# A diffusion layer with recurrence, long convolution and experts: equal column pieces, and gates as single fp32 products

## The chip, the cores and the metric

One core of one Trainium2 chip. The time is device microseconds (us) of one execution, the median of three: 927.65 us for the kernel before (925.95 to 929.68). Engines: PE multiplies matrices (its weight loads are shown as PEld), DVE and ACT work on elements, POOL too, SP issues the transfers (DMA).

## The reference

One layer over 512 latent tokens and 256 context tokens of width 1024, all in fp32:

- RMSNorm with shift and scale from the conditioning, then a projection into two head groups.
- A bidirectional gated recurrence over 512 channels. Two gates, r and i, are sigmoids of 64x64 block products of the convolved input u. With `log_a = -8 * r * softplus(-lam)`: `a = exp(log_a)`, `b = sqrt(-expm1(2 * log_a)) * (i * u)`, and the state is `h = a * h + b`, forward and backward, first over the context, then over the latents.
- A Hyena group: two long convolutions, done as transforms.
- Norms, an output projection, a gated residual, and a second RMSNorm.
- A mixture of experts: top group of 4, in it the top 2 of 8 experts; each expert is `(silu(t @ w_gate) * (t @ w_up)) @ w_down`, with 1024 x 512 weights. Then a residual and the last RMSNorm.

## The kernel before

The program is written in one order and recorded; a planner (`Recorder.order`) then lays every instruction on its engine by a list schedule with costs of its own, 25 passes, and keeps the order with the shortest planned end. So the order on an engine isn't that of the source, and a change of a few instructions lays all of it out anew. Copies and simple products may be put on one of two engines (`X`, the class `Either`). Buffers are fixed in the order of the source: an arena of 103 cells of 256 columns (`take`), and 12 slots of 2048 columns for rounded operands (`takeR`); `give` returns them.

Ahead of the experts stand, in the planner's order: filters, the conditioning products (`mod_group`, 32 columns wide), the norm, the recurrence (`lru_pair`, twice, for two blocks of 128 channels each), gelu, the convolutions (`order`, `long_conv`), the output projection and the routing.

In `lru_pair` the gates need more accuracy than one fp32r product gives, so weights and input are split into a rounded part and a remainder (`lwH`, `lwL`, and `st`, named `vst`), and each product is three fp32r products. There are 16 gates (4 blocks, 2 directions, r and i), each in two parts of 256 and 512 columns. The square root of 1 - a^2 comes from tanh: `ncoef` scales r so that 1 - a^2 = tanh(..) * (1 + a^2), and `q` holds a^2.

The experts are sorted by load; each gets a fixed number of places (`CAPS`: three of 64, then 192, 128, 128, 96, nine of 64, fifteen of 32, one of 0). A unit packs chunks of 64 or 32 tokens side by side into the 128 columns of PE: two 64s, four 32s, or, mixed, one 64 and two 32s. Two of the units are mixed: the one of the expert with 96 places (its chunks of 64 and 32, and another expert's 32; the last H of `ORDER = "MMHMQHQAMHQ"`, behind two units that are put first), and the last M. A is a group of two units of two 64s; Q is a unit of four 32s. In `product` each piece is one fp32 product per step, on its strip of columns; an order edge (`before`) keeps the pieces of a unit in sequence in the plan:

```
for i, (k, kk, h) in enumerate(parts):
    for (p0, w), wv in zip(sub[0], sub[2]):
        o = T.matmul(b[p0:p0 + w, :nc_], lhs[:, k, p0:p0 + w], wv(m, kk, h)[:, c0:c0 + nc_], ...
```

A unit has 8 steps of gate, 8 of up and 4 of down for each of two halves of the output. Before them its tokens are gathered (bf16 products with `R`), behind them the result is scattered and added to `x2`. The weights come in loads of 1 MB (`load`, issued at L1818 on the queue of SP) into a ring of buffers, in the order of use, six loads an expert; a load waits until PE has done with what its buffer held. The first three experts don't depend on the routing, all others do (`eid`).

Of the kernel before, what the change touches and what calls it, by code (L numbers as in the profile page):

```python
# [13 lines left out]
F32 = mybir.dt.float32  # L14
# [4 lines left out]
OP = mybir.AluOpType  # L19
# [658 lines left out]
class Arena:  # L678
# [9 lines left out]
    def take(self, name, shape, top=False, step=1):  # L688
        n = math.prod(shape)
        m = -(-n // 256)  # L690
        best = None
        for o in range(0, self.n - m + 1, step):
            if any(self.used[o:o + m]):
                continue
            key = -o if top else (max(self.stamp[o:o + m]), o)
            if best is None or key < best[0]:
                best = (key, o)
        if best is None:
            raise RuntimeError(f"arena: no room for {name} ({m} cells), {self.used.count(False)} free; "
                               + ", ".join(f"{k}@{o}+{c}" for k, (o, c) in self.live.items()))  # L700
        o = best[1]
        self.used[o:o + m] = [True] * m
        self.peak = max(self.peak, sum(self.used))
        self.clock += 1
        key = f"{name}.{self.clock}"
        self.live[key] = (o, m)
        v = View.of(self.mem)[:, o * 256:o * 256 + n]
        if len(shape) > 1:
            names = "abcdef"[:len(shape)]
            v = v.rearrange(f"p ({' '.join(names)}) -> p {' '.join(names)}", **dict(zip(names, shape)))  # L710
        v.key, v.home, v.since = key, self, max(self.stamp[o:o + m])
        return v
# [30 lines left out]
def kernel(ctx: ExitStack, tc: tile.TileContext, a: dict, out: bass.AP, dbg=None):  # L743
# [29 lines left out]
    take = AR.take  # L773
# [5 lines left out]
    def give(*vs):  # L779
        for v in vs:  # L780
            v.home.give(v)
# [7 lines left out]
    def ps():  # L789
        if REC.direct:  # L790
            nbank[0] += 1
            return View.of(Mem((128, 512), F32, banks[nbank[0] % 8]))
        return View.of(Mem((128, 512), F32, bank=-1))
# [382 lines left out]
    V.tensor_scalar(t8[0], t8[0], 0.0, 0.5, op0=OP.max, op1=OP.mult)  # L1176
    V.tensor_tensor(t8[4], t8[4], t8[0], op=OP.add)
    V.tensor_scalar(coef, t8[4], -16.0, None, op0=OP.mult)
    V.tensor_scalar(ncoef, t8[4], 16.0, None, op0=OP.mult)


    def split(src, wh, wl):

        X.copy(wh, src)
        X.tensor_tensor(wl, src, wh.bitcast(F32), op=OP.subtract)
# [27 lines left out]
    for i in range(2):  # L1213
# [3 lines left out]
        for h in range(2):  # L1217
            split(st[:, 2 * h:2 * h + 2], *(w[:, 2 * h:2 * h + 2] for w in UW[i]))
        give(st)
    lwH, lwL = (takeR("lw", [16, 128]) for _ in range(2))  # L1220
    split(lw, lwH, lwL)
    give(lw)
    ct = [take("ct", [512]) for _ in range(2)]
    for j in range(2):
        b = ps()
# [7 lines left out]
    give(*cH, *cL)  # L1233

    def lru_pair(blks):
        vs, sts = {}, {}
        for bk in blks:
            bc = ps()
            for j in range(2):
                T.transpose(bc[:, 128 * j:128 * j + 128], ct[j][:, 128 * bk:128 * bk + 128], ident)  # L1240
            bl = ps()
            for k in range(8):
                wh, wl = (w[:, k % 4, 128 * bk:128 * bk + 128] for w in UW[k // 4])
                h, l = (t[k // 4][:, k % 4] for t in (hH, hL))
                T.matmul(bl, wh, h, start=k == 0, stop=False)
                T.matmul(bl, wh, l, start=False, stop=False)
                T.matmul(bl, wl, h, start=False, stop=k == 7)
            v = take("v", [768])
            for b, o0, n in ((bc, 0, 256), (bl, 256, 512)):
                X.copy(v[:, o0:o0 + n], b[:, :n], bias=col("cab", bk), scale=col("caw", 8 + bk))  # L1250
                for k, d0, s0, m in ((0, 2, 0, n - 2), (1, 1, 0, n - 1), (3, 0, 1, n - 1)):
                    V.scalar_tensor_tensor(v[:, o0 + d0:o0 + d0 + m], b[:, s0:s0 + m], col("caw", 4 * k + bk),
                                           v[:, o0 + d0:o0 + d0 + m], op0=OP.mult, op1=OP.add)
            vs[bk] = v
        if blks[-1] == 3:
            give(*UW[0], *UW[1], *ct)
        for bk, v in vs.items():
            st = sts[bk] = takeR("vst", [2048], late=True)
            X.copy(st[:, :768], v)
            X.tensor_tensor(st[:, 768:1536], v, st[:, :768].bitcast(F32), op=OP.subtract)  # L1260
        its = [(bk, d) for bk in blks for d in range(2)]
        rt, it = {}, {}
        for bk, d in its:
            for m, (dst, bn) in enumerate(((rt, "ba"), (it, "bx"))):
                g = take("g", [768])
                gi = (d * 2 + m) * 4 + bk
                b1, b2 = ps(), ps()
                for b, c0, n in ((b1, 0, 256), (b2, 256, 512)):
                    for j, (w, o) in enumerate(((lwH, 0), (lwH, 768), (lwL, 0))):
                        T.matmul(b[:, :n], w[:, gi], sts[bk][:, o + c0:o + c0 + n], start=j == 0, stop=j == 2)  # L1270
                S.activation(g[:, :256], b1[:, :256], AF.Sigmoid, bias=col(bn, 4 * d + bk))
                S.activation(g[:, 256:], b2, AF.Sigmoid, bias=col(bn, 4 * d + bk))
                dst[bk, d] = g
        give(*sts.values())
        at, bt = {}, {}
        for bk, d in its:
            X.tensor_tensor(it[bk, d][:], it[bk, d][:], vs[bk][:], op=OP.mult)
        give(*vs.values())
        for bk, d in its:
            at[bk, d] = take("at", [768])  # L1280
            S.activation(at[bk, d][:], rt[bk, d][:], AF.Exp, scale=coef[:, 4 * d + bk:4 * d + bk + 1])
            S.activation(rt[bk, d][:], rt[bk, d][:], AF.Tanh, scale=ncoef[:, 4 * d + bk:4 * d + bk + 1])
            q = take("q", [768])
            X.tensor_tensor(q[:], at[bk, d][:], at[bk, d][:], op=OP.mult)
            V.scalar_tensor_tensor(rt[bk, d][:], q[:], 1.0, rt[bk, d][:], op0=OP.add, op1=OP.mult)
            give(q)
        for bk, d in its:
            S.activation(rt[bk, d][:], rt[bk, d][:], AF.Sqrt)
            X.tensor_tensor(rt[bk, d][:], rt[bk, d][:], it[bk, d][:], op=OP.mult)
        for bk in blks:  # L1290
            hf, hb = it[bk, 0], it[bk, 1]
            A_, B_ = at[bk, 0], rt[bk, 0]
            V.tensor_tensor_scan(hf[:], A_[:], B_[:], 0.0, op0=OP.mult, op1=OP.add)
            A_, B_ = at[bk, 1], rt[bk, 1]
            V.tensor_tensor_scan(hb[:, 255::-1], A_[:, 255::-1], B_[:, 255::-1], 0.0, op0=OP.mult, op1=OP.add)
            V.tensor_tensor_scan(hb[:, 767:255:-1], A_[:, 767:255:-1], B_[:, 767:255:-1], hb[:, 0:1],
                                 op0=OP.mult, op1=OP.add)
            X.tensor_tensor(rnn[:, bk], hf[:, 256:], hb[:, 256:], op=OP.add)
        for bk, d in its:
            give(rt[bk, d], it[bk, d], at[bk, d])  # L1300
# [177 lines left out]
    while left:  # L1478
        k = left.pop(0)
        i = int(k[1:] or 0)  # L1480
        if k[0] == "L":
            lru_pair((i, i + 1))
            if not [x for x in left if x[0] == "L"]:
                give(lwH, lwL)
        elif k[0] == "M":
            (mod_second, mod_third)[i - 1]()
        elif k[0] in "vab":
            project(*{"v": ("v", 1024, 0), "a": ("g0", 1536, 4), "b": ("g1", 2048, 8)}[k[0]], i)
        elif k[0] in "CD":
            order("CD".index(k[0]), i)  # L1490
            if not [x for x in left if x[0] in "CD"]:
                give(dff, dfi)
        elif k == "W":
            for h in range(WOE):
                wos[h, 0] = load_wo(h, 0)
        elif k == "X":
            load_x2()
        elif k[0] == "G":
            gelu_pair((i, i + 1))
        if not [x for x in left if x[0] in "LvabG"] and k[0] in "LvabG":  # L1500
            give(*hH, *hL)
# [350 lines left out]
    def expert_units(subs, need=lambda m: None, then=lambda: None, last=False):  # L1852
# [16 lines left out]

        def product(sub, m, lhs, parts, c0=0, nc_=512):  # L1870
            b, before = ps(), None
            for i, (k, kk, h) in enumerate(parts):
                for (p0, w), wv in zip(sub[0], sub[2]):
                    o = T.matmul(b[p0:p0 + w, :nc_], lhs[:, k, p0:p0 + w], wv(m, kk, h)[:, c0:c0 + nc_], start=i == 0,
                                 stop=i == len(parts) - 1, tile_position=(0, p0), skip_group_check=True)
                    if not REC.direct:

                        if before is not None:
                            o.preds.setdefault(before, None)
                        before = o.i  # L1880
            return b
# [155 lines left out]
```

## Time and profile before

| | |
|---|---|
| median of three runs | 927.65 us (925.95 to 929.68) |
| profiled execution | 931.36 us; its span 929.6 us |
| busy share of PE, DVE, ACT, POOL | 92%, 55%, 30%, 3% |
| moved by DMA | 259.73 MB, mean 279 GB/s |
| mean granted clock of PE | 0.971 |

A row of a group view names the line (that of a helper here: L560 for all plain operations, L567 for those that may go to either engine), the engine, the operation, output and inputs, for PE rows and columns of the weights, then the shape and the count; behind the bar the busy time in us, the mean of one in ns, and the idle time before them. An fp32 product on PE leaves two records in the trace, an fp32r or bf16 product one. Records of fp32r carry f32 in the view; those on slots with 128x128 weights are fp32r.

### The profile page before, as it was taken

The numbers are of one execution on the slowest core, as the hardware profiler recorded it, in microseconds if no ns is written. First come the engines' busy times: TensorE is split into PE (matmuls) and PEld (weight loads), VectorE is DVE, ScalarE is ACT, GpSimd is POOL, SyncE is SP. The second block draws the span as 40 slices with busy tenths as digits, with TensorE's granted clock in tenths as the row PEclk, the third lists the DMA queues.
The fourth block names the chain that finished last, engine by engine and source line by source line (L and its number), as shares of the span: only waits on it lengthen the run. The fifth ranks groups of instructions, "written<-read, shape, count | busy, mean of one in ns | idle before, by whom it ended". The sixth has DMA issues, their size and how long they took to land.

```text
span 929.6 us, 13429 instructions
## 1 busy us (share of the span) xinstructions
PE 855.6 (92%) x5282; PEld 453.6 (49%) x5283; DVE 507.3 (55%) x971; ACT 279.9 (30%) x511; POOL 23.6 (3%) x25
## 2 busy tenths in 40 slices
PE   3988998899999799599999999999999999999984
PEld 0344674578887577435544444453554323233332
DVE  7989889599999977604233322431413214212135
ACT  4678188764345124301211110120110100000014
POOL 0000001010003000000000000000000000000002
PEclk9989999799999899799999999999999999999997
DMA  9985377333423596398999989999999999876693
GB/s 292 414 276 195 103 238 218 135 118 120 148 80 131 187 327 223 119 361 306 367 386 386 386 294 359 388 386 386 386 387 386 386 387 382 321 281 223 231 335 142
DMA packets 132618, 259.73 MB, mean 279 GB/s; under 512 B 6928, under 2 KB 28432, under 8 KB 129606
## 3 DMA queue, kind: packets, MB, share of 16 engines
q1 hardware_dynamic: 132534, 258.81, 77.7%
q8 instruction: 43, 0.70, 0.3%
q14 instruction: 25, 0.20, 0.1%
q10 hardware_dynamic: 16, 0.02, 0.0%
HBM read 252.49 MB, written 6.31 MB: 278 GB/s over the span
## 4 chain that ended last, share of the span: by engine, by line
PE 68%; DVE 7%; DMA 1%; ACT 1%; issue 0%; SPq 0%; DVEq 0%; ACTq 0%
PE bank L560 68%; DVE arena L567 2%; DVE slot L567 2%; DVE arena L560 2%; DMA slot<-in_w_down_dram 1%; DVE slot L560 1%; ACT slot L560 0%; DVE R L560 0%; DVE rsb_in L560 0%; DVE fine L560 0%; ACT arena L560 0%; ACT slot L567 0%; SPq L1818 0%; DVE finy L560 0%; DVE hy L560 0%
## 5 line engine op out<-in xcount | busy, mean ns | idle before, releaser
L560 PE MATMUL bank<-arena 128*64 128x512 f32 (+8 forms) x1434 | 314.6, 533 | 26.0 <-DMA arena<-in_b_ada_dram 5.9
L560 PE MATMUL bank<-slot 128*128 128x512 f32 (+1 forms) x1064 | 282.8, 410 | 14.9 <-DVE slot L567 4.8
L560 PE MATMUL bank<-slot,arena 128*64 128x512 f32 (+2 forms) x936 | 242.9, 597 | 1.9 <-DMA slot<-in_w_down_dram 0.9
L560 PEld LDWEIGHTS bank<-slot 128*128 128x128 f32 x1064 | 195.2, 193 | 99.5 <-issue 27.3
L560 PEld LDWEIGHTS bank<-arena 128*32 128x32 f32 (+5 forms) x1434 | 100.5, 132 | 166.8 <-issue 117.5
L560 DVE TENSOR_TENSOR arena<-arena,bank 128x512 f32<-128x512 f32 (+2 forms) x131 | 80.5, 663 | 167.4 <-PE bank L560 167.2
L567 DVE TENSOR_TENSOR arena<-arena 128x512 f32<-128x512 f32 (+3 forms) x142 | 120.6, 886 | 2.5 <-DMA arena<-in_w_dram 1.8
L560 PEld LDWEIGHTS bank<-slot,arena 128*64 128x64 f32 (+1 forms) x936 | 58.3, 124 | 111.6 <-issue 101.0
L560 ACT ACTIVATE arena<-bank 128x512 f32<-128x512 f32 (+1 forms) x66 | 38.3, 595 | 243.4 <-PE bank L560 240.8
L560 PEld LDWEIGHTS <-slot 128*128 128x128 bf16 x1344 | 76.9, 98 | 40.9 <-issue 40.6
L560 PE MATMUL bank<-R,slot 128*128 128x128 bf16 x1344 | 88.7, 220 | 0.3 <-ACT arena L567 0.3
L567 DVE TENSOR_SCALAR arena<-bank,A2c,B2c 128x128 f32<-128x128 f32 x36 | 14.6, 410 | 115.6 <-PE bank L560 115.5
L567 ACT ACTIVATE arena<-bank,B2c,A2c 128x128 f32<-128x128 f32 x76 | 30.7, 454 | 137.1 <-DVE arena L567 85.4
L560 ACT ACTIVATE slot<-arena 128x512 fp32r<-128x512 f32 (+2 forms) x43 | 27.7, 645 | 113.5 <-DVE arena L560 104.2
L560 DVE SCALAR_TENSOR_TENSOR arena<-bank,iw,arena 128x512 f32<-128x512 f32 (+1 forms) x29 | 21.2, 732 | 69.6 <-PE bank L560 69.2
L560 PE MATMUL bank<-ident,arena 128*128 128x128 f32 (+2 forms) x234 | 40.7, 292 | 5.2 <-ACT arena L567 2.2
L560 ACT ACTIVATE arena<-arena 128x512 f32<-128x512 f32 (+6 forms) x59 | 32.7, 589 | 26.5 <-DVE arena L560 21.4
L560 PEld LDWEIGHTS bank<-ident,arena 128*128 128x128 f32 (+2 forms) x234 | 30.2, 160 | 19.9 <-issue 5.7
L567 ACT ACTIVATE slot<-slot 128x1024 fp32r<-128x1024 f32 (+1 forms) x32 | 26.4, 846 | 28.4 <-DVE slot L567 22.9
L567 DVE TENSOR_TENSOR slot<-slot 128x1024 fp32r<-128x1024 f32 (+1 forms) x35 | 33.7, 974 | 0.1
L560 ACT ACT_TABLE_LOAD x23 | 29.5, 1283 | 6.0 <-DMA arena<-in_pack_dram 4.6
L560 DVE TENSOR_TENSOR arena<-bank,arena 128x512 f32<-128x512 f32 (+1 forms) x42 | 27.7, 680 | 5.5 <-PE bank L560 3.1
(172 smaller groups left out, 417.3 us busy)
## 6 DMA issues: line engine op xcount, KB each, us to landing
arena<-in_w_down_dram SPq DMA_DIRECT2D x41, 1024.0 KB, 13.5
slot<-in_w_up_dram SPq DMA_DIRECT2D x39, 1024.0 KB, 14.0
slot<-in_w_gate_dram SPq DMA_DIRECT2D x32, 1024.0 KB, 13.6
arena<-in_w_gate_dram SPq DMA_DIRECT2D x30, 1024.0 KB, 11.8
arena<-in_w_up_dram SPq DMA_DIRECT2D x23, 1024.0 KB, 9.4
slot<-in_w_down_dram SPq DMA_DIRECT2D x20, 1024.0 KB, 10.3
arena<-in_w_ada_dram SPq DMA_DIRECT2D x32, 512.0 KB, 5.1
slot<-in_w_ada_dram SPq DMA_DIRECT2D x8, 1024.0 KB, 11.1
```

The costliest lines, as they stand in the source:

```text
L560: return self.rec.add(self.name, lambda: f(*[real(v) for v in args], **{k: real(v) for k, v in kw.items()}), outs, ins, cost, **x)
L567: return cost, lambda: f(*[real(v) for v in args], **{k: real(v) for k, v in kw.items()}), port
```

## The change

Three things. In `product` the pieces of a unit are cut to the width of its narrowest piece (`one`), so a 64-wide piece in a mixed unit becomes two 32-wide ones with the same weights. In the recurrence the square of the decay goes: with `ncoef` of half the size, 1 - a^2 = tanh(..) * (1 + a)^2, so the root is that of the tanh alone and (1 + a) is multiplied in behind it. And the gates are single fp32 products of `lw` and `v`, without splits; `lw` stays in the arena until the second pair is done.

```diff
-    V.tensor_scalar(ncoef, t8[4], 16.0, None, op0=OP.mult)
+    V.tensor_scalar(ncoef, t8[4], 8.0, None, op0=OP.mult)
...
-    lwH, lwL = (takeR("lw", [16, 128]) for _ in range(2))
-    split(lw, lwH, lwL)
-    give(lw)
...
-        for bk, v in vs.items():
-            st = sts[bk] = takeR("vst", [2048], late=True)
-            X.copy(st[:, :768], v)
-            X.tensor_tensor(st[:, 768:1536], v, st[:, :768].bitcast(F32), op=OP.subtract)
...
-                    for j, (w, o) in enumerate(((lwH, 0), (lwH, 768), (lwL, 0))):
-                        T.matmul(b[:, :n], w[:, gi], sts[bk][:, o + c0:o + c0 + n], start=j == 0, stop=j == 2)
+                    T.matmul(b[:, :n], lw[:, gi], vs[bk][:, c0:c0 + n], start=True, stop=True)
...
-            q = take("q", [768])
-            X.tensor_tensor(q[:], at[bk, d][:], at[bk, d][:], op=OP.mult)
-            V.scalar_tensor_tensor(rt[bk, d][:], q[:], 1.0, rt[bk, d][:], op0=OP.add, op1=OP.mult)
-            give(q)
         for bk, d in its:
             S.activation(rt[bk, d][:], rt[bk, d][:], AF.Sqrt)
+            V.scalar_tensor_tensor(rt[bk, d][:], at[bk, d][:], 1.0, rt[bk, d][:], op0=OP.add, op1=OP.mult)
...
+            one = min(w for _, w in sub[0])
+            turns = [(p, one, wv) for (p0, w), wv in zip(sub[0], sub[2]) for p in range(p0, p0 + w, one)]
             for i, (k, kk, h) in enumerate(parts):
-                for (p0, w), wv in zip(sub[0], sub[2]):
+                for p0, w, wv in turns:
```

## Rows read from the trace of the kernel before

**Rows 1.** The page: busy time and share of each engine; GB/s in 40 slices.

```profile
PE 855.6 (92%) x5282; PEld 453.6 (49%) x5283; DVE 507.3 (55%) x971; ACT 279.9 (30%) x511; POOL 23.6 (3%) x25
...
GB/s 292 414 276 195 103 238 218 135 118 120 148 80 131 187 327 223 119 361 306 367 386 386 386 294 359 388 386 386 386 387 386 386 387 382 321 281 223 231 335 142
```

**Rows 2.** Windows: busy us (x instructions) of each engine, granted clock, DMA share, GB/s.

```profile
700.00:780.00 80.00, 79.70 (x384) 27.32 (x381) 21.00 (x43) 7.47 (x13) 0.00 (x0) 1.00 1.05 386
780.00:910.00 130.00, 126.72 (x709) 41.34 (x708) 33.94 (x59) 11.85 (x24) 0.00 (x0) 1.00 0.80 286
```

**Rows 3.** Waits of the load queue, 780 to 912 us: total, times, longest.

```profile
SPq L1818 <- PE bank L560: 97.3, 18, 11.5
```

**Rows 4.** The chain that ended last: start us, us, what; its tail.

```profile
776.25 119.12 PE bank L560 x630
...
896.49 10.68 DMA slot<-in_w_down_dram
...
907.21 6.96 PE bank L560 x63
```

**Rows 5.** PE groups by form, 799.9 to 815.7 us: busy us, mean ns, idle.

```profile
L560 PE MATMUL bank<-arena 128*32 128x512 f32 x24 | 8.4, 604 | 0.0
L560 PE MATMUL bank<-arena 128*64 128x512 f32 x8 | 4.3, 618 | 0.0
L560 PE MATMUL bank<-slot,arena 128*64 128x512 f32 x8 | 4.3, 618 | 0.0
L560 PE MATMUL bank<-slot,arena 128*32 128x512 f32 x8 | 4.2, 604 | 0.0
```

**Rows 6.** The same view, 585.6 to 593.4 us, a unit of four.

```profile
L560 PE MATMUL bank<-slot,arena 128*32 128x512 f32 x40 | 7.9, 593 | 0.0
L560 PE MATMUL bank<-arena 128*32 128x512 f32 x32 | 7.1, 594 | 0.0
```

**Rows 7.** Windows ahead of the experts (columns as in Rows 2).

```profile
100.00:160.00 60.00, 58.35 (x362) 39.11 (x360) 52.94 (x78) 39.22 (x55) 2.40 (x1) 1.00 0.61 192
160.00:220.00 60.00, 51.78 (x244) 38.65 (x244) 50.56 (x54) 35.34 (x47) 3.25 (x2) 0.89 0.41 140
220.00:300.00 80.00, 78.79 (x369) 66.02 (x367) 77.41 (x96) 36.93 (x62) 9.32 (x5) 1.00 0.33 112
300.00:367.00 67.00, 60.13 (x274) 47.33 (x274) 56.55 (x106) 21.02 (x48) 1.91 (x1) 0.92 0.67 234
367.00:385.00 18.00, 5.14 (x62) 3.88 (x61) 17.34 (x65) 5.95 (x10) 0.19 (x1) 0.67 0.72 256
```

**Rows 8.** Groups by form on DVE, 100 to 210 us.

```profile
L567 DVE TENSOR_TENSOR arena<-arena 128x768 f32<-128x768 f32 x24 | 21.9, 950 | 0.3 <-ACT arena L560 0.2
...
L567 DVE TENSOR_TENSOR slot<-arena,slot 128x768 fp32r<-128x768 f32 x4 | 3.8, 950 | 0.0
...
L567 DVE TENSOR_TENSOR slot<-arena,slot 128x2048 fp32r<-128x2048 f32 x1 | 2.3, 2284 | 0.0
...
L567 DVE CAST slot<-arena 128x768 fp32r<-128x768 f32 x3 | 1.7, 560 | 0.0
...
L567 DVE CAST slot<-arena 128x2048 fp32r<-128x2048 f32 x1 | 1.2, 1226 | 2.0 <-DMA arena<-in_lw_dram 2.0
```

**Rows 9.** Groups by form on PE, 129.2 to 134.9 us: dense fp32r products.

```profile
L560 PE MATMUL bank<-slot 128*128 128x512 f32 x25 | 5.9, 394 | 0.0
```

**Rows 10.** Groups by form, whole run, on PE.

```profile
L560 PE MATMUL bank<-arena 128*128 128x256 f32 x128 | 31.7, 395 | 3.6 <-DVE arena L567 3.6
...
L560 PE MATMUL bank<-arena 128*128 128x512 f32 x48 | 24.0, 605 | 0.3 <-ACT arena L567 0.3
...
L560 PE MATMUL bank<-slot 128*128 128x256 f32 x48 | 9.9, 295 | 1.8 <-ACT arena L560 1.8
```

**Rows 11.** Waits of PE, 80 to 384 us: total, times, longest.

```profile
PE bank L560 <- DMA arena<-in_w_ada_dram: 5.3, 5, 2.5
PE bank L560 <- DVE arena L567: 4.2, 3, 3.0
```

More of the change, by code (lines that the diff above doesn't have):

```diff
@@ L1235, in lru_pair @@
     def lru_pair(blks):
-        vs, sts = {}, {}
+        vs = {}
         for bk in blks:
@@ L1273, in lru_pair @@
                 dst[bk, d] = g
-        give(*sts.values())
-        at, bt = {}, {}
+        at = {}
         for bk, d in its:
@@ L1483 @@
             if not [x for x in left if x[0] == "L"]:
-                give(lwH, lwL)
+                give(lw)
         elif k[0] == "M":
```

## The prediction

> **What bounds the kernel now.** I read the page first, then windows, the waits of the load queue, the chain, and last the groups of the two places that the change touches. PE is busy for 92% of the span [rows 1], but that is an average over two stages with different limits.
>
> The experts (the last stage, behind the routing) need PE and the weight stream together. From 700 to 780 us PE is busy for 79.7 of 80 us while the DMA engines move 386 GB/s; from 780 to 910 us PE is still busy (126.7 of 130 us), but the stream is down to 286 GB/s [rows 2]. The page's GB/s line holds 386 or 387 for whole runs of slices in this stage, and dips to 223 near the end [rows 1]. So up to 780 us the stream runs at its top; after that something holds it back. The load queue says what: in 780 to 912 us it waits 97.3 us for PE [rows 3], that is, for the matmuls that still read the buffer that the next load is to fill. The chain agrees: PE alone from 776 to 895 us, then the last weights (10.7 us), then 7.0 us of PE [rows 4]. The end of the kernel is set by a slow PE, which starves its own loads.
>
> Why PE is slow there: between 799.9 and 815.8 us it runs only one mixed unit (pieces of 64, 32 and 32 tokens). The view shows 16 records with 64 columns and 32 records with 32 columns in 15.8 us [rows 5]. One fp32 product leaves two records, so these are eight steps (one 64-wide and two 32-wide products each): 1.98 us a step. The 64 and the pair of 32s don't run beside each other: each half of a step takes 0.99 us. A unit of four 32-token pieces leaves 72 records in 7.8 to 7.9 us [rows 6]: eight records a step, nine steps, 0.88 us a step for four products.
>
> Before the experts the work is balanced: in 100 to 160 us PE is busy 58.4 and DVE 52.9 of 60 us, in 160 to 220 us 51.8 and 50.6, in 220 to 300 us 78.8 and 77.4 of 80 [rows 7]. Neither alone is the limit.
>
> **Equal pieces.** The lists in the code make two mixed units: the last one with M (one chunk of 64 and two 32s) and the H made of the expert with 96 places. Each has 8 steps of gate, 8 of up and 4 of down for each of two halves: 24; together 48 steps. Now 48 x 1.98 = 95 us of PE. With `one` = 32 the 64-wide piece becomes two 32-wide products on the same weights, so a step is four strips of 32, as in the unit of four: 48 x 0.88 = 42 us. PE gives back 53 us. All other units have one width already and keep their instructions. Added: 48 products, that stand in strips which ran empty, so no time is put on them.
>
> What it is worth is less, because the stream is next. 286 GB/s over 130 us, moved at 386 GB/s, takes 130 x 286/386 = 96 us: the last weights can land 34 us earlier and no more. The saving of PE (53 us) covers this with 19 us to spare, so I take **-34 us**. Bounds: 0 (the buffers still hold the loads back) and -53 (PE's whole saving, were the stream no limit). Late next: the weights of the last unit, four experts, for which PE will now stand still.
>
> That standing still has a price. Granted clock falls where PE idles: 0.67 over 367 to 385 us, in which PE was busy 5.1 of 18 us, and 0.89 over 160 to 220 us [rows 7]. [...] While weights arrive this hides under them (four loads of 1 MB at 386 GB/s take 10.9 us; four steps at half clock 7 us). The 7.0 us of PE after the last weights [rows 4] would take up to 14. Bounds 0 and +7; I take **+4 us**, the middle, since the clock can rise again during a last dense stretch.
>
> [...]
>
> **The recurrence.** All of it lies between 100 and 205 us. What goes from DVE: eight of the 24 products on 128x768 (the squares, 0.95 each, 7.6 us), four remainders of `vst` on 128x768 (3.8), the remainder of `lw` (2.3), its copy (1.2) and three copies of `v` (1.7) [rows 8]: 16.6 us. The fourth copy, on ACT, is under a microsecond. The scalar_tensor_tensor stays, behind the square root instead of before it. DVE's wait for the root isn't new (the product waited for it); now two operations stand behind it in place of one, and behind them the product, the scans and what else the planner puts there. The chain from tanh to scan is shorter by the square. Cost of the move: between -0.95 and +0.95 us (one such operation) for each of the two pairs of blocks; I take nothing, as DVE has other work to put ahead.
>
> What PE gets: 16 gates, each now three fp32r products of 512 columns and three of 256. 25 fp32r products with 512 columns take 5.9 us [rows 9], 0.24 each; the 48 of 256 take 9.9 us with what they overlap [rows 10], 0.21 at most, half of 0.24 at least. So 48 x (0.24 + 0.12 to 0.21) = 17 to 22 us now. As fp32: 24 products of 512 columns leave 48 records and take 24.0 us, 64 of 256 take 31.7 us [rows 10]: 1.00 and 0.50 us. 16 x 1.50 = 24 us. PE gains 2 to 7 us of work; I take +7.
>
> Beside what: PE is full in 100 to 160 us (58.4 of 60), so the 7 us are on the path there. But from 100 to 367 us PE idles 18 us in all (1.6, 8.2, 1.2 and 6.9 in four stretches [rows 7]). 5.3 us of its waits are for conditioning weights, which don't change, 4.2 for one kind of DVE product [rows 11]. With DVE ahead by up to 16.6 us the waits for DVE should go, in 300 to 367 us above all. End of the routing: between +7 (all on PE, nothing recovered) and -11 (7 us of work against all 18 us of idle time). I take **-4 us**, a little to the good side of the middle. It passes through in full, as the stream can start on the routed experts only after the routing.
>
> Buffers: the two slots of `lwH`, `lwL` and two of `vst` come free, `lw` keeps 8 cells of the arena until the last gates. Bounds: inside the range just given, since the only thing that freed slots can do is start `w_in` loads sooner, and cells kept can delay a load of the same stage. No wait on another engine is added beyond that, and no DMA is moved past another by hand. The planner lays out the whole order anew; I put nothing on that.
>
> **Sum.** Of the profiled execution's own time: 931.36 - 34 + 4 - 4 = 897.4 us. It stands 3.7 us above the median of the three runs (927.65), so on their scale 893.7; I write 893.
>
> **Rivals.**
> - Ring not free in time: before the mixed M comes A with two units of two 64s, and its last steps and scatter run beside the first steps of the mixed unit. If its buffers come free late, half of the 34 us stays: 893 + 17 = 910. For it: the stream begins to falter at 780 us, when the first mixed unit is half done. Against: up to there, with a PE busy 79.7 of 80 us, no load came late [rows 2]. 15%.
> - More before the experts: PE's idle goes whole, -11 instead of -4: 886. For: DVE loses 16.6 us in a stage where both engines are close to full. Against: 7 us more on PE just where it is full. 17%.
> - Slower: the four strips run one after the other. Place: the steps of the mixed units, on the path from 776 us on. Price: 4 x 0.88 = 3.5 us a step, 48 x (3.5 - 1.98) = 73 us: 928 - 4 + 73 = about 997. It decides as soon as a step costs over 1.98 us. Against: the unit of four strips has 0.88 us [rows 6]. What differs is only that two strips read the same weights. 4%.
> - The equal pieces do nothing: PE is slow at the end for another reason, and only the recurrence moves, 928 - 4 + 0: 924, inside what a measurement can't tell. 4%.
> - My forecast: 60%, with its own range 888 to 903.
>
> **How the numbers follow.** Down: -11 before the experts and no price for the clock (893 - 7 - 4 = 882), less 4 us for the spread of runs. Up: nearly to half of the gain (910). Left out are the last two rivals and the far end of the first: 878 to 909. About 0.5% (4.6 us) is what a measurement of this kernel can tell from no change. Faster 0.92 (the forecast, the first two rivals), same 0.03, slower 0.05 (the slower rival and a little for an order that goes wrong).
>
> **What would show it.** Right: no stretch of the mixed units with 64-wide records, 0.88 us a step; GB/s at 386 from about 450 us to the last weights; PE idle and waiting for `w_down` or `w_up` in the last 50 us, with a granted clock below 1 there; the end of routing between 370 and 390 us. Wrong: a load queue that still waits tens of microseconds for PE after the mixed M; steps over 1 us; a routing that ends 10 us later.

## The result, and the profile after

The changed kernel takes **888.41 us** (median of 4 runs, 888.2 to 889.56) against 928.52 us before (4 runs, 925.95 to 929.68): ratio of the means 0.9574, with a 95% interval of 0.9551 to 0.9598. The forecast was 893 us. The profiled execution took 888.55 us with a span of 886.8 us, 42.8 us below the profiled execution before (931.36 us). The medians are 40.1 us apart: the profiled execution before was 2.8 us slower than its median, the one after only 0.1.

The page answers to [rows 1]: busy us and share, then the granted clock and GB/s in 40 slices of 22.2 us. The line of GB/s now holds 384 to 389 from the 26th slice to the last but one; the dip to 223 is gone. The dips in slices 20, 24 and 25 (273, 347, 300) are still there; [rows 1] has them as 306, 294 and 359 in its slices 19, 24 and 25, which are a little longer.

```profile
PE 817.6 (92%) x5346; PEld 444.5 (50%) x5347; DVE 490.6 (55%) x954; ACT 284.7 (32%) x517; POOL 13.7 (2%) x18
...
PEclk9999999999999979699999999999999999999987
...
GB/s 294 414 263 352 183 163 279 72 95 143 106 72 131 119 357 199 239 225 387 273 389 386 386 347 300 389 386 386 386 387 386 387 386 387 386 386 386 387 384 133
```

Windows of the experts, as in [rows 2] (busy us of PE, PEld, DVE, ACT, POOL, then clock, DMA share, GB/s). First the whole stage, from the end of the routing to the last weights, then two stretches with dips, then its end. In 770 to 866 us PE is busy for 86 of 96 us and the stream is at 384 GB/s: the limit has changed hands. In 840 to 860 us PE stands still for 7 of 20 us and its granted clock is 0.83 on the mean: 0.50 from 846.0 to 852.8 us and 1.00 in the rest. A 32-wide record takes 1061 ns on the mean at 0.50 (847 to 852 us) and 596 ns at 1.00 (858 to 861 us). From 863 us on, when the last wait for weights is over, the clock is at 1.00.

```profile
372.00:866.00 494.00, 482.73 (x3656) 219.19 (x3656) 152.08 (x310) 65.97 (x133) 0.97 (x4) 0.99 1.00 365
420.00:440.00 20.00, 20.00 (x120) 8.15 (x117) 3.17 (x5) 1.19 (x2) 0.00 (x0) 1.00 0.77 273
520.00:540.00 20.00, 20.00 (x127) 7.76 (x124) 1.55 (x3) 1.65 (x3) 0.00 (x0) 1.00 0.95 335
540.00:560.00 20.00, 20.00 (x144) 10.10 (x144) 9.26 (x20) 4.17 (x9) 0.00 (x0) 1.00 0.83 300
690.00:770.00 80.00, 79.71 (x494) 31.66 (x495) 25.78 (x51) 8.37 (x15) 0.00 (x0) 1.00 1.05 387
770.00:866.00 96.00, 86.13 (x689) 34.07 (x682) 28.03 (x49) 9.93 (x19) 0.00 (x0) 0.96 1.04 384
840.00:860.00 20.00, 13.12 (x68) 2.97 (x65) 0.69 (x1) 0.60 (x1) 0.00 (x0) 0.83 1.05 386
863.00:871.70 8.70, 8.55 (x72) 4.88 (x73) 4.15 (x8) 4.08 (x10) 1.31 (x2) 1.00 0.47 162
```

In the kernel before the whole stage had 522 us of PE in 527 us and 344 GB/s, and PE behind its last wait for weights ran at 1.00 too:

```profile
383.00:910.00 527.00, 522.23 (x3572) 221.06 (x3571) 153.47 (x312) 66.97 (x136) 0.97 (x4) 1.00 0.94 344
...
907.20:914.20 7.00, 6.99 (x64) 3.62 (x65) 3.49 (x7) 4.06 (x10) 2.58 (x3) 1.00 0.34 121
```

The waits of the load queue from 770 to 866 us answer to [rows 3] (total, times, longest): 39.4 us in 96 us, instead of 97.3 in 132, and no wait over 4.1 us.

```profile
SPq L1807 <- PE bank L560: 39.4, 21, 4.1
```

The waits of PE from 800 to 870 us are new, and name the weights of the last unit:

```profile
PE bank L560 <- DMA arena<-in_w_up_dram: 4.3, 3, 1.7
PE bank L560 <- DMA arena<-in_w_down_dram: 2.7, 2, 1.7
```

The chain (start, us, what) answers to [rows 4]. Its first row starts where the routing hands over to the experts; in the kernel before that row was `383.13 232.22 PE bank L560 x1760`. PE's last long wait for weights is over at 863.15 us (907.21 before), and 8.5 us of PE stand behind it (7.0 before), with 70 records instead of 63. One more load lands after that, at 865.8 us (910.1 before).

```profile
372.05 233.49 PE bank L560 x1760
...
849.15 13.95 DMA arena<-in_w_down_dram
...
863.15 8.49 PE bank L560 x70
```

PE by form from 797.5 to 801.0 us, inside a mixed unit, answers to [rows 5]: only 32-wide records, 32 of them in 3.6 us. At eight records a step that is 0.90 us, where it was 1.98.

```profile
L560 PE MATMUL bank<-slot,arena 128*32 128x512 f32 x32 | 3.6, 595 | 0.0
```

Ahead of the experts, windows that answer to [rows 7]. Between 160 and 220 us PE is now busy for 57.4 us at a clock of 0.97 (51.8 and 0.89 before). The 16 us of the routing itself, 356 to 372 us, are as long as before.

```profile
100.00:160.00 60.00, 58.34 (x323) 32.44 (x322) 45.87 (x64) 41.87 (x57) 0.00 (x0) 1.00 0.63 204
160.00:220.00 60.00, 57.42 (x246) 45.19 (x244) 52.98 (x66) 42.04 (x58) 5.02 (x1) 0.97 0.29 99
```

Forms that answer to [rows 8] (DVE, 90 to 210 us) and [rows 10] (PE, whole run): eight products on 128x768 fewer, and the gates as single fp32 products among the x80 and the x160.

```profile
L567 DVE TENSOR_TENSOR arena<-arena 128x768 f32<-128x768 f32 x16 | 14.7, 952 | 13.4 <-ACT arena L560 13.4
```

```profile
L560 PE MATMUL bank<-arena 128*128 128x512 f32 x80 | 40.2, 611 | 3.0 <-ACT arena L567 2.3 <-ACT arena L560 0.6
L560 PE MATMUL bank<-arena 128*128 128x256 f32 x160 | 40.0, 384 | 2.0 <-DVE arena L567 1.8 <-ACT arena L560 0.2
```

### The profile page after: what moved, and what is told of

Read it like the earlier page. It is cut to its first block, busy times and chain, and to the rows that moved or that the text cites. A ratio compares the mean times of both kernels' runs of the same rounds, so it can differ in the third digit from the quotient of the medians.

```text
span 886.8 us, 13538 instructions
## 1 busy us (share of the span) xinstructions
PE 817.6 (92%) x5346; PEld 444.5 (50%) x5347; DVE 490.6 (55%) x954; ACT 284.7 (32%) x517; POOL 13.7 (2%) x18
## 4 chain that ended last, share of the span: by engine, by line
PE 73%; DVE 13%; DMA 6%; ACT 5%; SPq 2%; issue 1%; ACTq 0%
PE bank L560 73%; DVE arena L567 6%; DVE arena L560 3%; DVE slot L567 3%; ACT arena L560 2%; DMA arena<-in_w_ada_dram 2%; DMA arena<-in_w_down_dram 2%; SPq L1807 1%; ACT L560 1%; DMA arena<-in_c_delta_dram 1%; DVE slot L560 1%; DMA gd<-arena 1%; DMA arena<-in_x_dram 1%; ACT arena L567 1%; SPq L560 0%
## 5 line engine op out<-in xcount | busy, mean ns | idle before, releaser
L560 PE MATMUL bank<-arena 128*32 128x512 f32 (+7 forms) x1530 | 308.0, 530 | 28.2 <-ACT arena L560 11.0
L560 PE MATMUL bank<-slot 128*128 128x512 f32 x968 | 269.2, 418 | 7.0 <-ACT slot L560 2.6
L560 PEld LDWEIGHTS bank<-slot 128*128 128x128 f32 x968 | 178.1, 191 | 90.6 <-issue 30.7
L560 PE MATMUL bank<-slot,arena 128*32 128x512 f32 (+2 forms) x1000 | 207.6, 598 | 0.8 <-ACT arena L560 0.7
L560 PEld LDWEIGHTS bank<-arena 128*32 128x32 f32 (+4 forms) x1530 | 106.5, 133 | 160.9 <-issue 100.7
L560 DVE TENSOR_TENSOR arena<-arena,bank 128x512 f32<-128x512 f32 (+2 forms) x131 | 80.4, 663 | 152.2 <-PE bank L560 152.0
L567 DVE TENSOR_TENSOR arena<-arena 128x512 f32<-128x512 f32 (+3 forms) x138 | 116.2, 872 | 19.9 <-ACT arena L560 15.1
L560 ACT ACTIVATE arena<-bank 128x512 f32<-128x512 f32 (+1 forms) x66 | 38.4, 596 | 228.3 <-PE bank L560 228.2
L560 PEld LDWEIGHTS bank<-slot,arena 128*32 128x32 f32 (+1 forms) x1000 | 54.6, 122 | 90.1 <-issue 82.3
L560 PEld LDWEIGHTS <-slot 128*128 128x128 bf16 x1344 | 78.2, 99 | 42.0 <-issue 41.6
L560 PE MATMUL bank<-R,slot 128*128 128x128 bf16 x1344 | 90.3, 222 | 0.3 <-ACT arena L567 0.3
L560 ACT ACTIVATE slot<-arena 128x512 fp32r<-128x512 f32 (+2 forms) x43 | 27.5, 644 | 105.0 <-DVE arena L560 91.2
L560 DVE SCALAR_TENSOR_TENSOR arena<-bank,iw,arena 128x512 f32<-128x512 f32 (+1 forms) x29 | 21.2, 732 | 55.3 <-PE bank L560 55.0
L560 PE MATMUL bank<-ident,arena 128*128 128x128 f32 (+2 forms) x234 | 39.8, 288 | 9.1 <-DVE slot L560 4.9
L560 PEld LDWEIGHTS bank<-ident,arena 128*128 128x128 f32 (+2 forms) x234 | 28.7, 156 | 25.1 <-issue 5.8
L560 ACT ACTIVATE arena<-arena 128x512 f32<-128x512 f32 (+6 forms) x59 | 32.9, 590 | 23.8 <-DVE arena L560 17.0
L560 DVE TENSOR_TENSOR arena<-bank,arena 128x512 f32<-128x512 f32 (+1 forms) x42 | 27.3, 679 | 1.6 <-PE bank L560 1.5
## 6 DMA issues: line engine op xcount, KB each, us to landing
slot<-in_w_up_dram SPq DMA_DIRECT2D x38, 1024.0 KB, 14.2
arena<-in_w_up_dram SPq DMA_DIRECT2D x24, 1024.0 KB, 13.9
```

The lines of the kernel that those rows point to most:

```text
L560: return self.rec.add(self.name, lambda: f(*[real(v) for v in args], **{k: real(v) for k, v in kw.items()}), outs, ins, cost, **x)
L567: return cost, lambda: f(*[real(v) for v in args], **{k: real(v) for k, v in kw.items()}), port
```

## The experiments

For every kernel three times are read from its profiled execution: the end of the routing (where the chain's row of the hand-over starts), the landing of the last load of expert weights, and the end. Their distances separate what the parts do.

| kernel | median us | ratio, 95% interval | routing ends | to the last weights | after them |
|---|---|---|---|---|---|
| before (trace) | 928.52 | 1 | 383.1 | 527.0 | 19.5 |
| the change | 888.41 | 0.9551 to 0.9598 | 372.0 | 493.8 | 21.0 |
| e1 pieces only | 890.05 | 0.9568 to 0.9603 | 374.4 | 495.2 | 18.3 |
| e2 recurrence only | 919.96 | 0.9885 to 0.992 | 371.9 | 523.1 | 22.2 |
| e3 gates only | 909.9 | 0.9763 to 0.9799 | 366.3 | 523.0 | 22.0 |
| e4 square only | 921.92 | 0.9879 to 0.9936 | 374.5 | 527.4 | 17.9 |
| e5 change, all units in 32s | 889.87 | 0.9555 to 0.9596 | 374.2 | 491.3 | 22.0 |
| e6 change, two gather planes | 881.97 | 0.947 to 0.9502 | 373.2 | 487.0 | 21.1 |
| e7 change, Q third | 882.12 | 0.9473 to 0.9505 | 372.7 | 486.4 | 21.0 |
| e8 before, other order | 923.99 | 0.9918 to 0.9962 | 376.4 | 526.3 | 19.5 |
| e9 before, other order | 912.26 | 0.9816 to 0.9864 | 364.7 | 520.4 | 25.4 |
| e10 change, other order | 887.01 | 0.9536 to 0.9585 | 370.9 | 492.4 | 21.9 |
| e11 gates only, other order | 919.72 | 0.9899 to 0.9948 | 371.9 | 525.4 | 19.7 |
| e12 gates, pieces, Q third | 873.39 | 0.9401 to 0.9454 | 361.0 | 486.5 | 22.6 |

Ratios are to the kernel before in the same batch (928.96 us for e1 to e4, 929.65 for e5 to e8, 926.49 for e9 to e12). What lies behind the last weights is 17.9 to 25.4 us in the kernels with mixed units and 18.3 to 22.6 in those with equal pieces.

**The parts alone.** e1 has only this edit, in `product`:

```diff
+            one = min(w for _, w in sub[0])
+            turns = [(p, one, wv) for (p0, w), wv in zip(sub[0], sub[2]) for p in range(p0, p0 + w, one)]
-                for (p0, w), wv in zip(sub[0], sub[2]):
+                for p0, w, wv in turns:
```

> Only the equal pieces; the recurrence as before. My theory: PE lagging in the two mixed units starved the weight stream, and the stream is the next limit. Then the routing stays at 383 us, the last weights land 33 us earlier (910 to 877 us) and the time is 928.5 - 33 + 1.5 (slower PE at the end) = 897 us. Rival (PE's whole saving counts, the stream is no limit): 928.5 - 53 = 876 us. Rival (the recurrence carries most of the gain): 915 us or more.

It took 890.05 us. From the routing to the last weights it needs 31.8 us less than before, and its load queue waits for PE about as long as in the change (770 to 870 us):

```profile
SPq L1818 <- PE bank L560: 39.0, 20, 3.9
```

That is the experts' share, shown without the rest. But the time also fell by some 7 us more than was expected, and these lie ahead of the experts, where the program is the same as before: the routing ends at 374.4 us instead of 383.1. This was the first sign that the order alone is worth microseconds.

e2 is the change without that edit.

> Only the recurrence (gates as single fp32 products, no square); mixed units as before. My theory: the routing ends 11 us earlier, as in the changed kernel, and all of that passes through: 917.5 us, the mixed steps still at 1.98 us. Rival (the 11 us are the luck of a new order): routing anywhere within 5 us of 383, time 924 to 933 us. Rival (what is gained ahead of the routing is lost in the experts): routing at 372, time 925 us or more.

919.96 us: 2.5 above the number expected. The routing ends at 371.9 us, as in the change, and the experts' stage stays near its old length (523.1). e1 gives 38.9 us and e2 gives 9.0 us; both together, in the change, give 40.1. The parts don't add, since e1 already had most of the earlier routing.

e3 keeps the square, with `ncoef` and `q` as before, and has only the gates; e4 has only the square:

```diff
...
-    split(lw, lwH, lwL)
...
-                        T.matmul(b[:, :n], w[:, gi], sts[bk][:, o + c0:o + c0 + n], start=j == 0, stop=j == 2)
+                    T.matmul(b[:, :n], lw[:, gi], vs[bk][:, c0:c0 + n], start=True, stop=True)
```

```diff
-    V.tensor_scalar(ncoef, t8[4], 16.0, None, op0=OP.mult)
+    V.tensor_scalar(ncoef, t8[4], 8.0, None, op0=OP.mult)
...
-            q = take("q", [768])
-            X.tensor_tensor(q[:], at[bk, d][:], at[bk, d][:], op=OP.mult)
-            V.scalar_tensor_tensor(rt[bk, d][:], q[:], 1.0, rt[bk, d][:], op0=OP.add, op1=OP.mult)
...
+            V.scalar_tensor_tensor(rt[bk, d][:], at[bk, d][:], 1.0, rt[bk, d][:], op0=OP.add, op1=OP.mult)
```

> Only the gates as single fp32 products, without splits; the square and the mixed units as before. If DVE's work decides: 9 us less on DVE against up to 7 us more on PE, a gain of 2 to 3 us, 926 us. If the freed buffers (two for the split weights, two for the split inputs) decide: most of the 11 us, 919 us. If PE's extra work decides: 932 us or more.

> Only the square of the decay taken out; gates split as before, mixed units as before. If DVE's work decides: 7.6 us less on DVE and nothing more on PE, a gain of 5 to 8 us, 922 us. If the freed buffers decide: no gain, 928 us within 2.

e4 landed on its first number (921.92), which after what follows may be chance. e3 missed all of its numbers: 909.9 us, 19 us faster than before, and its routing ends at 366.3 us, 5.7 us earlier than in e2, which removes more work. A smaller edit that gives more than the larger one which contains it can't be explained by the cost of the operations alone.

**The order alone.** The planner takes, among the instructions that could start within `LOOK` ns of the first, the one of the highest priority. Changing this one number changes no instruction and lays all of them out anew:

```diff
-LOOK = 50
+LOOK = 60
```

e8 does this to the kernel before, e10 to the change, e11 to e3; e9 is the kernel before with 40.

> The kernel before with one constant of the planner changed (LOOK 60 in place of 50), so the same work in another order: the scatter of planning. If orders scatter by less than the gain of the recurrence: routing within 3 us of 383, time within 4 us of 928.5. If the 11 us ahead of the routing can be luck: a shift of 8 us or more either way.

> The kernel before with LOOK 40: one more order of the same work. Two other orders of it (the equal pieces alone, and LOOK 60) ended the routing at 374.4 and 376.4 us, where the kernel before has 383.1. If the order before is an unlucky one: routing at 373 to 379 us, time 920 to 925. If the two others were lucky: routing at 381 to 386 us, time 927 to 932.

> The changed kernel with LOOK 60: one more order of its work. Four orders so far (itself, every unit in 32s, two planes, Q third) ended the routing at 372.0 to 374.2 us. If the work sets this: routing at 370 to 376 us, time 886 to 892 us. If orders scatter as widely as those of the kernel before: a routing outside 370 to 376.

> The single fp32 gates alone (square and mixed units as before), with LOOK 60. With LOOK 50 their routing ended at 366.3 us, against 371.9 with the square gone as well. If the gates by themselves are worth more than both parts together: routing at 365 to 369 us, time 908 to 914. If 366.3 was a lucky order: routing at 371 to 378 us, time 915 to 923.

The same work as in the kernel before has its routing done at 376.4 us (e8, between its two theories) and at 364.7 us (e9, further than either theory had it); in time these orders are 5.7 and 14.2 us faster than the kernel before in their batches. So the kernel before was one of four orders of one work: 383.1, 374.4 (e1), 376.4 and 364.7 us, 18 us apart, and it was the worst of them.

For the work of the change, e10 came out as its first theory had it (887.01 us, routing at 370.9). The other traces add less than the expectation of e10 says: ahead of the experts the change, e2, e6 and e7 run one and the same order, but for a handful of neighbouring instructions, and end the routing at 372.0, 371.9, 373.2 and 372.7 us. With e5 (374.2) and e10 these are three orders, 3 us apart. The means of the orders are 374.7 for the old work and 372.5 for the new: 2 us of difference, beside a scatter of 18 among the old ones. e3's early routing was such an order too: with `LOOK` at 60 the same kernel (e11) ends it at 371.9 us and takes 919.72 us, the second theory of e11.

Where the order before lost its time, by windows, first the kernel before, then e1, with the same instructions ahead of the experts:

```profile
160.00:180.00 20.00, 16.12 (x94) 9.39 (x93) 10.70 (x14) 13.26 (x17) 0.00 (x0) 0.83 0.47 155
...
100.00:220.00 120.00, 110.13 (x605) 77.76 (x604) 103.49 (x131) 74.56 (x101) 5.64 (x3) 0.94 0.51 166
```

```profile
160.00:180.00 20.00, 19.31 (x117) 14.19 (x117) 14.63 (x19) 17.72 (x25) 0.00 (x0) 1.00 0.61 192
```

And e9:

```profile
100.00:220.00 120.00, 116.81 (x675) 87.09 (x673) 112.67 (x146) 81.57 (x113) 2.97 (x1) 1.00 0.54 181
```

In 160 to 180 us the order before leaves PE idle for 3.9 us, and its granted clock is 0.83; e1 has 0.7 us of idle time and 1.00. Over 100 to 220 us PE is busy for 6.7 us more in e9 than in the kernel before. In the kernel before PE waits around there for conditioning weights above all, and DVE and ACT wait for PE (156 to 184 us: total, times, longest):

```profile
PE bank L560 <- DMA arena<-in_w_ada_dram: 3.7, 4, 2.5
DVE arena L567 <- PE bank L560: 9.3, 1, 9.3
ACT arena L560 <- PE bank L560: 9.6, 3, 4.8
```

**What the experts' stage still loses.** e5 asks whether it is the mixing of widths that cost time, or 64-wide strips as such: all units run in 32s.

```diff
-            one = min(w for _, w in sub[0])
+            one = 32
```

> The changed kernel with every unit cut into pieces of 32, also those of two 64s. My theory (four strips run side by side whether or not two of them read the same weights): a step of a former two-64 unit costs 0.88 us against 0.886, and the time stays at 888 within 4 us. Rival (strips that share weights get in each other's way, hidden in the changed kernel by the slack of PE): steps over 1 us, and as PE has no slack in 372 to 600 us, 10 us or more on top, 900 us.

889.87 us, no difference that can be measured. By form over the whole run the change has 864 records of 64 columns; e5 has none, and 1728 more of 32. First the change, then e5:

```profile
L560 PE MATMUL bank<-slot,arena 128*64 128x512 f32 x464 | 107.8, 598 | 0.0
L560 PE MATMUL bank<-arena 128*32 128x512 f32 x488 | 97.6, 620 | 5.8 <-DMA arena<-in_w_up_dram 4.3 <-DMA arena<-in_w_down_dram 1.1 <-ACT arena L567 0.3
L560 PE MATMUL bank<-slot,arena 128*32 128x512 f32 x504 | 95.2, 611 | 0.8 <-ACT arena L560 0.7
L560 PE MATMUL bank<-arena 128*64 128x512 f32 x400 | 92.8, 598 | 0.0
```

```profile
L560 PE MATMUL bank<-slot,arena 128*32 128x512 f32 x1432 | 204.6, 598 | 3.6 <-DMA slot<-in_w_up_dram 1.7 <-DMA slot<-in_w_ada_dram 1.3 <-ACT arena L560 0.7
L560 PE MATMUL bank<-arena 128*32 128x512 f32 x1288 | 193.6, 604 | 7.0 <-DMA arena<-in_w_up_dram 5.0 <-DMA arena<-in_w_down_dram 1.0 <-ACT arena L560 0.7
```

The rows overlap each other, since strips of both kinds run side by side, so their sums (393.4 and 398.2 us) count some time twice. PE's busy time from the routing to the last weights, which doesn't, is 477.4 us in e5 and 482.7 in the change: two strips of 64 and four strips of 32 take the same time for the same tokens, as far as can be told. So a 64-wide strip isn't slow; a step that holds both widths is (1.98 us against 0.90).

e6 takes work off PE in this stage: it leaves out the third bf16 plane of the gather, 448 of 1344 products.

```diff
-                        for m in range(3):
+                        for m in range(2):
```

> The changed kernel with two of the three bf16 planes gathered (the last plane of the tokens is left out of the sum). PE loses a third of its gather products, 14 units x 32 x 0.056 = 25 us. My theory (the stream is the limit from about 450 us on): the stream stalls of 14 us ahead of 560 us shrink, the rest is hidden: 876 to 888 us. Rival (PE is the limit still): 888 - 25 = 863 us or less.

881.97 us: 6.4 us for about 21 us less of busy PE (461.6 us from 373 to 860 us, against 482.7). Most of the PE time taken away is hidden behind the stream. Of the dips the one at 420 to 440 us is milder (366 GB/s instead of 273) and the one at 520 to 560 us is gone (387 and 386 instead of 335 and 300):

```profile
420.00:440.00 20.00, 20.00 (x140) 9.11 (x137) 3.64 (x7) 2.35 (x5) 0.00 (x0) 1.00 1.03 366
520.00:540.00 20.00, 20.00 (x154) 9.26 (x152) 5.06 (x13) 4.56 (x10) 0.00 (x0) 1.00 1.05 387
540.00:560.00 20.00, 20.00 (x114) 8.95 (x112) 6.66 (x11) 2.35 (x5) 0.00 (x0) 1.00 1.05 386
```

e7 attacks the dip at 520 to 560 us by the sequence of the units: Q, four experts with much weight and little PE, comes before the first H.

```diff
-ORDER = "MMHMQHQAMHQ"
+ORDER = "MMQHMHQAMHQ"
```

> The changed kernel with the units in the order MMQHMHQAMHQ in place of MMHMQHQAMHQ, so that a unit that needs much weight for its PE time (four experts) comes before the first H, which needs little. My theory: the stream no longer stalls at 420 to 440 and 520 to 560 us, where the load queue waits for PE; the last weights land up to 12 us earlier, 877 us. Rival (the stalls come from the start behind the routing, not from the H): no gain, 888 us. Rival (PE waits for the four experts' weights instead): slower, 895 us.

882.12 us: 486.4 us from the routing to the last weights, 7.4 less than the change, of the up to 12 expected. The dip at 520 to 560 us is gone, that at 420 to 440 us stayed, so the sequence explains one of them:

```profile
420.00:440.00 20.00, 20.00 (x117) 8.12 (x116) 3.55 (x6) 1.20 (x2) 0.00 (x0) 1.00 0.76 274
520.00:540.00 20.00, 20.00 (x229) 10.88 (x229) 7.28 (x18) 2.83 (x7) 0.00 (x0) 1.00 1.05 386
540.00:560.00 20.00, 20.00 (x197) 10.33 (x196) 6.34 (x15) 2.95 (x8) 0.00 (x0) 1.00 1.05 387
```

e12 joins what had proved best: the gates of e3 with the square kept, the equal pieces, and Q third.

> The best parts together: equal pieces, single fp32 gates with the square kept, units in the order MMQHMHQAMHQ. If the parts add: routing at 366 us, last weights 486 us behind it, then 21 us: a span of 873, 875 us in time. If 366.3 was a lucky order that this plan doesn't find again: routing at 371 to 376, 880 to 885 us.

It is the fastest of all, 873.39 us, 0.9428 of before and 15 us below the change, near the first of its two numbers. Of the 16.7 us between the spans of their profiled executions 7.3 lie in the stage, where Q is the change, and 11.0 ahead of the end of the routing, at 361.0 us; behind the last weights 1.6 are lost. The plan did find the order of e3 again: ahead of the experts the records of PE, DVE, ACT and POOL stand in the same sequence in both traces. So two profiled executions of one order end the routing 5.3 us apart, at 366.3 and 361.0 us; e3's was the slowest of its five (913.01 us, median 909.9). In the first 100 us e3 had the lower clock, first e3, then e12:

```profile
0.00:100.00 100.00, 78.89 (x407) 35.77 (x409) 87.31 (x233) 63.49 (x119) 7.37 (x11) 0.95 0.88 314
```

```profile
0.00:100.00 100.00, 78.67 (x423) 36.69 (x425) 89.77 (x235) 65.76 (x124) 7.45 (x12) 1.00 0.89 319
```

The early routing of e12 is thus that good order once more. Whether keeping the square helps isn't shown.

## Why the prediction was right

The difference of the two profiled executions, -42.8 us, splits into the three terms of the sum as -33.2 from the routing to the last weights, +1.5 behind the last weights, and -11.1 ahead of the routing's end. The prediction had -34, +4 and -4. Some 2.7 us of the -42.8 are the slow profiled execution before, and can't be placed in one of the three.

**Equal pieces, -34: right, in size and in reason.** The stage went from 527.0 to 493.8 us, and e1 alone gives 31.8. No luck of an order explains this: the seven kernels with mixed units take 520.4 to 527.4 us for it, and the four with equal pieces, the same units and the whole gather (the change, e1, e5, e10) take 491.3 to 495.2. Steps take 0.90 us; four strips, two of them with the same weights, do run side by side, and the rival with 997 us fell. The stream was next, as argued: the bytes of the stage (494 us x 365 GB/s, 180 MB) would need 467 us at 386 GB/s, and e6 shows that PE beyond that point gives little. The rival with a ring that isn't free in time fell too: the stream is at 384 GB/s up to the last weights. Tens of microseconds of queue waits were a sign of being wrong, but the 39 us found, in pieces of at most 4.1 us, do no harm. "No load came late" up to 780 us was wrong for the dips at 420 to 440 and 520 to 560 us, which both kernels have; e7 shows that one of them is the sequence of the units. PE's busy time in the stage fell by 39.5 us (522.2 to 482.7) and not by 53. At most 3.4 us of the difference are the slower clock near the end (an estimate: half of the 6.8 us that it spent at 0.50); the rest wasn't separated, and lay under the stream.

**The clock, +4: right that it falls, wrong that this costs anything at the end.** PE waits for `w_up` and `w_down` (7.0 us) and its clock is 0.83 in 840 to 860 us, as predicted. But it is back at 1.00 for the work behind the last wait (863 to 871.7 us), as before the change (907.2 to 914.2 us): the clock took nothing of the +7 there. The chain's last row of PE is 1.5 us longer because 70 records are left instead of 63. The +1.5 of the split isn't the clock's either, and e1, with the same equal pieces, has 18.3 us behind the last weights, less than the 19.5 before. The half clock of the estimate does occur: 0.50 from 846.0 to 852.8 us here, and in the kernel before in 165 to 171 and 375 to 383 us. But no run shows the +4, which was an estimate, the middle of 0 and +7: the trace has the fall among the waits, under loads at 386 GB/s, and 1.00 behind the last one.

**Ahead of the experts, -4: the term that was mis-sized; -11.1 was measured.** The prices of the operations held. The gates take 24.5 us of PE (16.2 and 8.3 more than in [rows 10]), for which 24 was written; of the three-product gates one row of 9.9 us is gone and another is 9.9 us shorter, so PE got some 4.7 more, inside the 2 to 7. DVE's busy time up to the routing fell by 16.4 us (343.3 to 326.9), for which 16.6 was written; in e5, the same work in another order, it is 333.8, since the planner puts some operations on other engines. What failed is the sentence "The planner lays out the whole order anew; I put nothing on that". PE's busy time up to the routing is the same in both profiled executions, 326.2 us, in spite of the longer gates; the lower clock before, 0.97 and 0.96 in the windows below against 1.00 and 0.97, can account for that, as an estimate (3% of 73.9 us and 1% of 249.1 us are 4.7 us). In this reckoning all of the 11.1 us is idle time. Of it 7.1 us lie ahead of 100 us, where PE now does 81.0 us of work instead of 73.9 and where no removed operation stood [rows 8]; 4.0 us lie between 100 us and the 16 us of the routing (idle 17.9 before, 13.9 after). First the kernel before, then the changed one:

```profile
0.00:100.00 100.00, 73.86 (x364) 34.39 (x366) 90.10 (x233) 64.23 (x125) 0.79 (x8) 0.97 0.79 280
100.00:367.00 267.00, 249.06 (x1246) 191.11 (x1244) 237.45 (x331) 132.51 (x210) 16.87 (x9) 0.96 0.50 167
```

```profile
0.00:100.00 100.00, 80.97 (x424) 37.08 (x426) 90.30 (x231) 68.74 (x131) 2.73 (x9) 1.00 0.89 316
100.00:356.00 256.00, 242.09 (x1154) 180.29 (x1152) 221.02 (x314) 133.27 (x210) 5.02 (x1) 0.97 0.47 159
```

And e1, e8 and e9 got 6.7 to 18.4 us out of a new order of unchanged work. So the rival "more before the experts" named the size (-11), but its reason, DVE's relief, isn't shown: most of the gain lies where nothing was relieved. What the new recurrence and the new gates are worth in themselves stays open; by the means of four and three orders it is about 2 us, which a scatter of 18 us between orders, and of 5 us between two executions of one order, doesn't let one call shown.

That the forecast came within 5 us is owed to the large term, and in part to luck. On the scale of the profiled executions it was 897.4 against 888.55, 8.9 us off; it came nearer because 3.7 us were taken off for the slow profiled execution before, and the one after was not slow. The small term's sign may be owed to the poor order before alone.

## What to carry to other kernels

Price a change of the bound engine by the next limit, not by its own saving: 53 us were in reach, the stream gave 34, and 33 came. Where a planner lays out all instructions, take a few orders of the unchanged kernel (one number of the planner is enough) before a gain of one or two per cent is put down to an edit, and compare the traces: two kernels may run the same order, and then they are one sample. And try the sequence of the units in a weight-bound stage: here one unit with much weight and little compute, moved ahead of one with much compute, gave 6 us.

## What the runs showed of the hardware that was not expected

Cutting 864 records of 64 columns into 1728 of 32 cost nothing that can be measured, neither in PE's busy time nor in the kernel's (e5). A step with both widths took 1.98 us, so its 64-wide half and its pair of 32s took 0.99 us each, more than a whole step of four equal strips (0.90). A PE whose clock was at 0.83 over 20 us ahead of the last weights was at 1.00 behind them, and the loads ran at 386 GB/s in those 20 us, so the slow stretch stayed hidden under them. And one order of the same instructions ahead of the experts, profiled in two kernels, took 5.3 us longer in the execution with the lower clock (0.95 against 1.00 in the first 100 us).
